# Decay differences of a Mamba-2 scan on GpSimd, one chunk ahead, with a third decay tile

## The chip, the core and the metric

One program on one core of one Trainium2 chip. The metric is the device time of one execution in microseconds, the median of several runs. The engines are named as in the profile: PE is TensorE, DVE is VectorE, ACT is ScalarE, POOL is GpSimd, SP is the engine that issues most DMAs. An engine works through its own queue in order; an instruction that waits holds up all that stands behind it on that engine.

## What is computed

A decoder of two layers over 2048 positions of width 1024: a Mamba-2 layer, then a layer of latent attention, with a final norm. The change lies in the chunked scan of the first layer (32 heads of 64 channels in 4 groups, 128 states, kernel chunks of 128 positions), cut from the reference to what matters:

```python
def step(state, inp):
    x_c, dt_c, B_c, C_c = inp
    cum = jnp.cumsum(dt_c * A_g, axis=1)
    seg = cum[:, :, None] - cum[:, None, :]
    L = jnp.exp(jnp.where(causal, seg, -jnp.inf))
    CB = jnp.einsum('btgn,bsgn->btsg', C_c, B_c)
    y_intra = jnp.einsum('btsg,btsgh,bsgh,bsghp->btghp', CB, L, dt_c, x_c)
    y_inter = jnp.einsum('btgn,bghpn,btgh->btghp', C_c, state, jnp.exp(cum))
    w_end = jnp.exp(cum[:, -1:] - cum) * dt_c
    new_state = state * jnp.exp(cum[:, -1])[..., None, None] + \
        jnp.einsum('bsgn,bsgh,bsghp->bghpn', B_c, w_end, x_c)
    return new_state, y_intra + y_inter
```

The kernel keeps the cumulated sums with the opposite sign. A decay tile holds, for one group and one chunk, the differences of 8 heads between each position (a partition) and each position (a column), clamped at zero, and then exp of minus that; the causal mask comes in through `CB`.

## The kernel before

The first layer runs over 4 blocks of 512 positions and, in each, over 4 groups; a group has 4 chunks of 128 positions, so there are 64 chunks. For one block and group there are three sweeps of matmuls over four PSUM banks each, all in fp16 pairs of a high and a low part, three matmuls a product: `xbc` (the inputs of the scan, with a convolution of width 4 that reads three columns of halo), `zgate` (the gate, in tiles `sz`) and `outp` (the output projection, one group later). The generator `ssd` makes the scan of one group. `mamba` runs the sweeps and, between their steps, 20 steps of `ssd`; the tile framework then puts the instructions in order by priority and its own model, and issues the waits. So a line's place in the code is not its place in an engine's queue.

What a sweep leaves in a PSUM bank has to be taken out before the next sweep may write there: for `xbc` ACT copies it to `craw` (L641), with the convolution behind (L645 on ACT, L647 on DVE, halo copies on POOL at L640 and L642); for `zgate` ACT makes a tanh (L670) and DVE multiplies (L671); for `outp` DVE adds into `hs` (L750).

In a chunk `ssd` does, as far as the change touches it:

- `decays` (L819) takes a tile `big` of 128 x 1024 fp32, of which there are two, and issues on SP the load of 8 rows of the cumulated sums, broadcast to all partitions (L825). The load for the next chunk is issued in the middle of a chunk.
- Eight operations on DVE (L893) subtract each position's own sum from the 128 columns of a head and clamp at zero.
- ACT makes the exponential of the whole tile (L897), DVE multiplies with `CB` (L898), and TensorE uses it in 32 small matmuls against `Xd` (L929). `Xd` is x times dt (DVE, L906).
- POOL makes the low halves of `Ct`, `Xp` and `Sp` (L846): `Ct` and `Xp` go into matmuls of the chunk, and `Sp`, the state, into those of the next chunk. DVE updates the state at L952 and L953.

Rows of a block's input come through `rows_in` (L596): two tiles `hx` of 128 x 1024 fp32 are loaded, normed, written as fp16 pairs into two more, and stored to `xp_d`; then the same for the other half. `fill` loads them back turned (eight transposing DMAs), and `steps` (L764 and behind) begins with matmuls on them. There are four `hx`. In the first block they also hold weights whose squares are summed (`scan`, through `later`), and `steps` takes one for itself.

Of the kernel before, what the change touches and what calls it, by code (L numbers as in the profile page):

```python
# [13 lines left out]
F16 = mybir.dt.float16  # L14
I32 = mybir.dt.int32
AF = mybir.ActivationFunctionType
ALU = mybir.AluOpType
# [4 lines left out]
P = 128  # L22
T = 2048
D = 1024
DI = 2048
G = 4
H = 32
# [3 lines left out]
NB = T // TB  # L31
KD = D // P
# [35 lines left out]
class Net:  # L68
# [273 lines left out]
    def mamba(self, cp):  # L342
# [7 lines left out]
        first = [self.t(self.sp, "big", [P, D], bufs=2) for _ in range(2)]  # L350
# [1 line left out]
        first += [self.t(self.sp, "yT", [P, D], bufs=4) for _ in range(4)]  # L352

        def later(kind):
            return self.t(self.hh, "hx", [P, D], bufs=4)

        def together(*parts):
            for group in zip_longest(*parts):
# [210 lines left out]
    def load_x(self, b, src):  # L569

        nc = self.nc
        self.xn[b] = xs = [self.t(self.hh, "hx", [P, D], bufs=4) for _ in range(4)]
        for i in range(4):
            nc.sync.dma_start(xs[i], src[i * P:(i + 1) * P, :])
        r = self.rows_rms(xs, [self.t(self.sp, "yt", [P, D], BF16, bufs=2) for _ in xs], D)
        for c in range(4):
            for i, x in enumerate(xs):
                v = x[:, c * D // 4:(c + 1) * D // 4]
                if i == 3:
                    nc.scalar.activation(v, v, AF.Copy, scale=r[:, i:i + 1])  # L580
                else:
                    nc.vector.tensor_scalar(v, v, r[:, i:i + 1], None, ALU.mult)
# [13 lines left out]
    def rows_in(self, b, src, tag="hx"):  # L596

        nc = self.nc
        for at in (0, 2 * P):
            xs = [self.t(self.hh, tag, [P, D], bufs=4) for _ in range(2)]  # L600
            for i, x in enumerate(xs):
                nc.sync.dma_start(x, src[at + i * P:at + (i + 1) * P, :])
            yield
            r = self.rows_rms(xs, [self.t(self.sp, "yt", [P, D], BF16, bufs=2) for _ in xs], D)
            up = self.t(self.sm, "rx", [P, 2], bufs=2)
            nc.vector.tensor_scalar(up, r, XSCALE, None, ALU.mult)
            us = [self.t(self.hh, tag, [P, KD, 2, P], F16, bufs=4) for _ in range(2)]
            for i, (x, u) in enumerate(zip(xs, us)):
                self.pair16(u[:, :, 0], u[:, :, 1], x.rearrange("p (k c) -> p k c", k=KD), up[:, i:i + 1])
            yield  # L610
            for i, u in enumerate(us):
                nc.sync.dma_start(self.xp_d[b][at + i * P:at + (i + 1) * P, :], u.rearrange("p k n c -> p (k n c)"))
# [144 lines left out]
    def steps(self, b):  # L757

        nc, v, xT = self.nc, self.nc.vector, self.xT[b]
        ps = self.t(self.pp, "tr", [P, TB], bufs=4)  # L760

        for k in range(KD):
            for n in range(2):
                nc.tensor.matmul(ps[0:2 * H, :], self.wdt[:, k].rearrange("p n h -> p (n h)"), xT[k][:, n, :],  # L764
                                 start=k + n == 0, stop=k + n == KD)
        wk = self.t(self.hh, "hx", [P, D], bufs=4)
        rt = self.t(self.sp, "yt", [2 * H, TB], bufs=2)
        nc.scalar.activation(rt, ps[0:2 * H, :], AF.Copy, scale=self.dtdown[0:2 * H])
        ps = self.t(self.pp, "tr", [P, TB], bufs=4)
# [4 lines left out]
        raw, e, q, p, dA, cT = (wk[:, n * P:n * P + P] for n in range(6))  # L774
# [44 lines left out]

    def decays(self, b, g, c):  # L820

        at, h0 = 16 * b + 4 * g + c, c * H + g * 8
        if at not in self.decay:
            E = self.decay[at] = self.t(self.sp, "big", [P, D], bufs=2)
            self.nc.sync.dma_start(E, self.dtv[b][5][h0:h0 + 8, :].rearrange("h t -> (h t)").partition_broadcast(P))  # L825
            return E
        return self.decay.pop(at).rearrange("p (h t) -> p h t", h=8)

    def ssd(self, b, g):

# [32 lines left out]
        for c in range(4):  # L863
            s = slice(c * P, (c + 1) * P)
            h0 = c * H + g * 8
# [11 lines left out]
                v.tensor_tensor(v8(t), v8(pi), heads(ecum), ALU.mult)  # L877
                return t

            if not (b or g or c):  # L880
                self.decays(0, 0, 0)
            E = self.decays(b, g, c)
            pb = self.t(self.pp, "tr", [P, TB], bufs=4)
            nc.tensor.transpose(pb[:, 0:P], BT[:, s], self.ident)
            nc.tensor.matmul(pb[:, P:2 * P], BT[:, s], CT[:, s], start=True, stop=True)
# [3 lines left out]
                Ct = halves(pair("Ct", P, 2), CT[:, s])  # L889
            CB = self.t(self.sp, "CB", [P, P], bufs=2)  # L890
            v.tensor_tensor(CB, pb[:, P:2 * P], self.triu, ALU.mult)
            for h in range(8):
                v.tensor_scalar(E[:, h, :], E[:, h, :], cum[:, h0 + h:h0 + h + 1], 0.0, ALU.subtract, ALU.max)  # L893
            after = 16 * b + 4 * g + c + 1
            if after < 16 * NB:
                self.decays(after // 16, after // 4 % 4, after % 4)
            act(E, E, AF.Exp, scale=-1.0)  # L897
            v.tensor_tensor(E, E, CB.unsqueeze(1).to_broadcast([P, 8, P]), ALU.mult)  # L898
            yield
# [12 lines left out]
            for h in range(8):  # L912
                hc = slice(h * 64, (h + 1) * 64)
                act(y[:, hc], px[:, hc], AF.Copy, scale=self.Dsk[:, g * 8 + h:g * 8 + h + 1])
            yield
            if b > 1 and c:
                yield
# [23 lines left out]
            yield  # L941
            if b == 1 and c:
                yield
            if not last:
                pst = self.t(self.pp, "tr", [P, TB], bufs=4)
                self.mm3(pst, Bt[:, 0], Bt[:, 1], Xp[:, 0], Xp[:, 1], True, True)
                if first:
                    st = self.state[g] = self.t(self.sp, f"st{g}", [P, TB], bufs=1)
                    v.tensor_copy(st, pst)
                else:  # L950
                    st = self.state[g]
                    v.tensor_tensor(v8(st), v8(st), heads(dec), ALU.mult)  # L952
                    v.tensor_tensor(st, st, pst, ALU.add)  # L953
                if c < 3:
                    old = halves(pair("Sp", TB, 1), st)
# [746 lines left out]
```

## Time and profile before

| | |
|---|---|
| median of 3 runs | 2904.24 us (2898.55 to 2908.7) |
| the profiled execution | 2901.06 us, its span 2899.3 us |
| the chip's granted TensorE clock | 0.992 of full speed |
| weights, input and start | 0 to 100 us |
| the scan with its projections | 100 to 1515 us |
| the second layer's projections | 1515 to 2010 us |
| attention | 2010 to 2620 us |
| last heads and output | 2620 to 2900 us |

The stages are cut by hand where the mix of work changes. POOL is busy for 301.57 us of the 1415 us of the scan, ACT for 878.65. A busy TensorE row counts a matmul from its start to its modelled end, and these overlap, so idle time is what a reader can trust. Idle time of another engine costs nothing by itself: it counts where TensorE waits for that engine.

### The profile page before, as it was taken

The page shows a single profiled execution, that of the slowest core. Times are in us where ns is not written, and L with a number is a line of the kernel's source. Part 1 is how long each engine was busy: PE and PEld are TensorE (multiplying, and loading weights), DVE is VectorE, ACT ScalarE, POOL GpSimd, SP SyncE. Part 2 cuts the span into 40 slices and gives each one's busy share as a digit, 9 for nine tenths or more (in the row PEclk, how much of TensorE's full clock was granted, in tenths as well). Part 3 has the DMA queues.
Part 4 walks back from the last instruction along what each step waited for, and adds up shares of the span by engine and source line. Part 5 has one row for each costly group of instructions (what it writes and reads, how often), then busy time and mean ns, then how long its engine had stood idle before and what let it go on. Part 6 is the DMA issues. An engine that isn't in the chain of part 4 may idle for free. (4 is left out here: it accounts for less than half of the span.)

```text
span 2899.3 us, 58091 instructions
## 1 busy us (share of the span) xinstructions
PE 2796.2 (96%) x21166; PEld 1621.4 (56%) x21166; DVE 2112.2 (73%) x5123; ACT 1801.4 (62%) x3900; POOL 853.5 (29%) x984
## 2 busy tenths in 40 slices
PE   7899999999999999998999999999999999998998
PEld 3455466544454454454455545555666666665787
DVE  6789877787777888788876355357777777778454
ACT  8767745576556665556554334234888888888522
POOL 0111212122122221123221122223665665665300
PEclk9999999999999999999999999999999999999999
DMA  8756636566665677647766877862212223223453
GB/s 287 258 191 202 217 116 194 166 197 170 203 208 163 194 201 225 215 143 211 229 143 232 269 217 230 243 200 78 70 50 67 65 53 73 68 64 89 164 200 109
DMA packets 358755, 483.33 MB, mean 167 GB/s; under 512 B 180162, under 2 KB 221922, under 8 KB 357028
## 3 DMA queue, kind: packets, MB, share of 16 engines
q1 hardware_dynamic: 347332, 443.70, 51.0%
q0 software_dynamic: 11136, 35.92, 3.5%
q8 instruction: 166, 2.72, 0.4%
q14 instruction: 121, 0.99, 0.1%
HBM read 332.83 MB, written 119.41 MB: 156 GB/s over the span
## 5 line engine op out<-in xcount | busy, mean ns | idle before, releaser
L1406 POOL TENSOR_TENSOR PTs<-x,PTs 128x512 f16<-128x512 f32 (+1 forms) x380 | 439.1, 1179 | 261.7 <-ACT PTs L1393 171.7
L1388 ACT ACTIVATE x<-s 128x512 f32<-128x512 f32 (+3 forms) x640 | 326.4, 524 | 48.7 <-PE s L1384 30.5
L84 PE MATMUL mm<-xT,wsp 128*128 128x512 f16 x800 | 306.1, 383 | 3.5 <-ACT wsp L115 3.3
L85 PE MATMUL mm<-xT,wsp 128*128 128x512 f16 x800 | 305.6, 382 | 0.0
L86 PE MATMUL mm<-xT,wsp 128*128 128x512 f16 x800 | 304.5, 381 | 0.2 <-DVE wsp L116 0.2
L1393 ACT ACTIVATE PTs<-x 128x1024 f16<-128x1024 f32 (+1 forms) x320 | 297.1, 929 | 9.4
L1271 DVE CUSTOM_DVE_ANT_0 junk<-s,fence,mx 128x512 bf16<-128x512 f32 (+1 forms) x372 | 242.1, 651 | 43.3 <-PE s L1269 3.0
L1423 PE MATMUL o<-K,PTs 128*128 128x65 f16 x2176 | 261.9, 192 | 2.0 <-POOL PTs L1406 1.5
L1421 PE MATMUL o<-K,PTs 128*128 128x64 f16 x2176 | 263.1, 192 | 0.0
L1422 PE MATMUL o<-K,PTs 128*128 128x65 f16 x2176 | 262.9, 194 | 0.0
L84 PE MATMUL mm<-wsp,xT 128*128 128x512 f16 (+1 forms) x640 | 231.9, 363 | 10.9 <-ACT craw L641 8.9
L85 PE MATMUL mm<-wsp,xT 128*128 128x512 f16 (+1 forms) x640 | 232.9, 364 | 3.3 <-DVE wsp L116 3.3
L846 POOL TENSOR_TENSOR Xp<-Xw,Xp 128x512 fp32r<-128x512 f32 x64 | 85.6, 1338 | 503.5 <-ACT Xp L845 346.4
L1421 PEld LDWEIGHTS <-PTs 128*128 128x128 f16 x2176 | 204.3, 96 | 52.2 <-issue 4.4
L86 PE MATMUL mm<-wsp,xT 128*128 128x512 f16 (+1 forms) x640 | 232.7, 364 | 0.0
L1422 PEld LDWEIGHTS <-PTs 128*128 128x128 f16 x2176 | 202.3, 97 | 52.8
L647 DVE SCALAR_TENSOR_TENSOR cacc<-craw,pack,cacc 128x512 f32<-128x512 f32 x288 | 213.7, 769 | 16.3 <-ACT cacc L645 15.1
L1382 PE MATMUL s<-xT,K 98*128 98x512 f16 (+1 forms) x628 | 218.5, 348 | 5.0 <-DVE mx L1271 3.9
L1383 PE MATMUL s<-xT,K 96*128 96x512 f16 (+1 forms) x628 | 218.3, 348 | 0.0
L1269 PE MATMUL s<-K,xT 96*128 96x512 f16 (+1 forms) x616 | 212.2, 347 | 6.1 <-DVE mx L1271 4.3
L1384 PE MATMUL s<-xT,K 96*128 96x512 f16 (+1 forms) x628 | 216.9, 345 | 0.0
L84 PE MATMUL mm<-wsp,yT 128*128 128x512 f16 (+1 forms) x512 | 199.9, 390 | 15.5 <-DVE sz L671 14.5
(476 smaller groups left out, 7111.5 us busy)
## 6 DMA issues: line engine op xcount, KB each, us to landing
wsp<-wi_d SPq DMA_DIRECT2D x96, 512.0 KB
big<-cumT SPq DMA_DIRECT2D x64, 512.0 KB
wraw<-in_ssm_w_out_dram SPq DMA_DIRECT2D x96, 256.0 KB
wi_d<-wsp SPq DMA_DIRECT2D x32, 512.0 KB
wsp<-wo_d SPq DMA_DIRECT2D x32, 512.0 KB
wsp<-wu_d SPq DMA_DIRECT2D x28, 512.0 KB
hx<-in_ssm_w_in_dram SPq DMA_DIRECT2D x48, 256.0 KB
wraw<-in_ssm_w_in_dram SPq DMA_DIRECT2D x48, 256.0 KB
```

The lines of the kernel that those rows point to most:

```text
L84: mm(out, l_hi, r_hi, start=start, stop=False)
L85: mm(out, l_hi, r_lo, start=False, stop=False)
L86: mm(out, l_lo, r_hi, start=False, stop=stop)
L1271: self.nc.vector.tensor_tensor_reduce(junk[:, :w], s[:, :w], fence[:, at:at + w], -1.0 / MSCALE, peak[:, i - 1, j:j + 1] if i else 3.0e38, ...
L1382: mm(s, K[0:98, 0, ks], Q[0:98, 0, c], start=True, stop=False)
L1383: mm(s, K[0:96, 0, ks], Q[0:96, 1, c], start=False, stop=False)
L1388: act(o, s, AF.Exp)
L1393: act(u[:, 0, at:end], x[:, at:end], AF.Copy)
L1406: engine.tensor_tensor(u[:, 1, a:b], x[:, a:b], u[:, 0, a:b], ALU.subtract)
L1421: mm(o[:, 0:64], hi, V[:, k, 0:64], start=k == 0 and j == 0, stop=False, skip_group_check=True)
L1422: mm(o[:, 0:65], hi, V[:, k, 64:129], start=False, stop=False, skip_group_check=True)
L1423: mm(o[:, 0:65], lo, V[:, k, 64:129], start=False, stop=k == 4 * qb + j, skip_group_check=True)
```

## The change

Three things change together.

1. `decays` takes a tile for chunk n, counted through all blocks and groups, from `big` (two tiles) or, for each third chunk, from a new tag `hE` (one tile). So there are three decay tiles in turn.
2. The eight differences go from DVE to POOL, into `differences`. The code calls it for the next chunk: four heads in the second step of the current chunk, four in its fourth. For the first chunks of block 0 and group 0 it is called at the start.
3. The space of `hE` comes from `hx`, which goes from four tiles to three. `load_x` takes three `hx` and the `hE`. `rows_in` allocates its output tiles one by one, so that the second can take the buffer of the first input.

```diff
         def later(kind):
-            return self.t(self.hh, "hx", [P, D], bufs=4)
+            return self.t(self.hh, "hx", [P, D], bufs=3)
...
-        self.xn[b] = xs = [self.t(self.hh, "hx", [P, D], bufs=4) for _ in range(4)]
+        self.xn[b] = xs = [self.t(self.hh, "hx", [P, D], bufs=3) for _ in range(3)]
+        xs.append(self.t(self.hh, "hE", [P, D], bufs=1))
...
         for at in (0, 2 * P):
-            xs = [self.t(self.hh, tag, [P, D], bufs=4) for _ in range(2)]
+            n = 3 if tag == "hx" else 4
+            xs = [self.t(self.hh, tag, [P, D], bufs=n) for _ in range(2)]
...
-            us = [self.t(self.hh, tag, [P, KD, 2, P], F16, bufs=4) for _ in range(2)]
-            for i, (x, u) in enumerate(zip(xs, us)):
+            us = []
+            for i, x in enumerate(xs):
+                u = self.t(self.hh, tag, [P, KD, 2, P], F16, bufs=n)
+                us.append(u)
...
     def decays(self, b, g, c):
 
-        at, h0 = 16 * b + 4 * g + c, c * H + g * 8
-        if at not in self.decay:
-            E = self.decay[at] = self.t(self.sp, "big", [P, D], bufs=2)
-            self.nc.sync.dma_start(E, self.dtv[b][5][h0:h0 + 8, :].rearrange("h t -> (h t)").partition_broadcast(P))
-            return E
-        return self.decay.pop(at).rearrange("p (h t) -> p h t", h=8)
+        h0 = c * H + g * 8
+        E = self.t(self.hh, "hE", [P, D], bufs=1) if (16 * b + 4 * g + c) % 3 == 2 else \
+            self.t(self.sp, "big", [P, D], bufs=2)
+        E = self.decay[b, g, c] = E.rearrange("p (h t) -> p h t", h=8)
+        self.nc.sync.dma_start(E.rearrange("p h t -> p (h t)"),
+                               self.dtv[b][5][h0:h0 + 8, :].rearrange("h t -> (h t)").partition_broadcast(P))
+
+    def differences(self, b, g, c, heads):
+
+        E, cum, h0 = self.decay[b, g, c], self.dtv[b][1], c * H + g * 8
+        for h in heads:
+            self.nc.gpsimd.tensor_scalar(E[:, h, :], E[:, h, :], cum[:, h0 + h:h0 + h + 1], 0.0, ALU.subtract, ALU.max)
...
-            if not (b or g or c):
-                self.decays(0, 0, 0)
-            E = self.decays(b, g, c)
+            if first and g == 0:
+                self.decays(b, g, c)
+                self.differences(b, g, c, range(8))
+            after = 16 * b + 4 * g + c + 1
+            after = (after // 16, after // 4 % 4, after % 4) if after < 16 * NB else None
+            E = self.decay.pop((b, g, c))
...
-            for h in range(8):
-                v.tensor_scalar(E[:, h, :], E[:, h, :], cum[:, h0 + h:h0 + h + 1], 0.0, ALU.subtract, ALU.max)
-            after = 16 * b + 4 * g + c + 1
-            if after < 16 * NB:
-                self.decays(after // 16, after // 4 % 4, after % 4)
+            if after:
+                self.decays(*after)
             act(E, E, AF.Exp, scale=-1.0)
...
                 act(y[:, hc], px[:, hc], AF.Copy, scale=self.Dsk[:, g * 8 + h:g * 8 + h + 1])
+            if after:
+                self.differences(*after, range(4))
             yield
...
             if b == 1 and c:
                 yield
+            if after:
+                self.differences(*after, range(4, 8))
```

What this makes of the engines' queues shows at one place, the end of `zgate` for block 2, group 2, while the scan is at group 1 (about 903 to 911 us of the profile). The numbers behind a name are the framework's; `big_10206` is one decay tile, that of chunk 1 of group 1, in both programs. DVE before, from a late difference to the first eviction of `sz`:

```order
L893 TENSOR_SCALAR big_10206<-big_10206,d_cum_8132 128x128
L245 SCALAR_TENSOR_TENSOR rsq_10143<-rsx_10129,rss_10141 128x4
L967 TENSOR_SCALAR pw_9176<-pw_9176 128x4
L893 TENSOR_SCALAR big_10206<-big_10206,d_cum_8132 128x128
L247 SCALAR_TENSOR_TENSOR rsy_10145<-rsq_10143,rsy_10139 128x4
L243 TENSOR_TENSOR rss_10147<-rsy_10145 128x4
L245 SCALAR_TENSOR_TENSOR rsq_10149<-rsx_10129,rss_10147 128x4
L247 SCALAR_TENSOR_TENSOR rsy_10151<-rsq_10149,rsy_10145 128x4
L968 SCALAR_TENSOR_TENSOR rr_10153<-rsy_10151,wod,pw_9176 128x4
L671 SCALAR_TENSOR_TENSOR sz_10091<-sz_10091,mm_9910 128x512
```

In the changed program the same small operations stand there without the differences. ACT at the same place before, and then the piece of its queue where this tile's exponential (L897 before, L907 now) stands after the change:

```order
L532 ACTIVATE yt_10107,hs_9439<-wraw_10002,pack 128x32
L115 ACTIVATE y_10062<-y_9940,pw_9176 128x4x128
L897 ACTIVATE big_10206<-big_10206 128x1024
L670 ACTIVATE sz_10091<-mm_9910,half 128x512
L670 ACTIVATE sz_10100<-mm_9911,half 128x512
```

```order
L645 ACTIVATE craw_9876<-mm_9639,down 128x512
L532 ACTIVATE yt_10010,hs_9439<-wraw_9928,pack 128x32
L907 ACTIVATE big_10206<-big_10206 128x1024
L653 ACTIVATE xs_9834<-cacc_9829 128x512
L645 ACTIVATE craw_9894<-mm_9640,down 128x512
```

The exponential of the tile has moved from ahead of the evictions of `sz` to ahead of the last eviction of `craw`, one sweep earlier. (Before, the exponential of the tile before it, `big_9866`, stands at that place.) POOL before and now, where the differences of this tile come:

```order
L846 TENSOR_TENSOR Xp_9672<-Xw_9661,Xp_9672 128x512
L846 TENSOR_TENSOR Ct_10193<-BC_9630,Ct_10193 128x128
L846 TENSOR_TENSOR Sp_9787<-st_197_1104,Sp_9787 128x512
L642 COPY halo<-craw_9817 128x3
L642 COPY halo<-craw_9835 128x3
```

```order
L856 TENSOR_TENSOR Xp_9672<-Xw_9661,Xp_9672 128x512
L856 TENSOR_TENSOR Ct_10201<-BC_9630,Ct_10201 128x128
L837 TENSOR_SCALAR big_10206<-big_10206,d_cum_8140 128x128 x8
L856 TENSOR_TENSOR Sp_9795<-st_197_1112,Sp_9795 128x512
L646 COPY halo<-craw_9825 128x3
```

All eight differences stand together, between `Ct` of one chunk and `Sp` of the chunk before it, and ahead of the halo copies.

More of the change, by code (lines that the diff above doesn't have):

```diff
@@ L765, in steps @@
                                  start=k + n == 0, stop=k + n == KD)
-        wk = self.t(self.hh, "hx", [P, D], bufs=4)
+        wk = self.t(self.hh, "hx", [P, D], bufs=3)
         rt = self.t(self.sp, "yt", [2 * H, TB], bufs=2)
```

## The prediction

> **What bounds the kernel now.** I read the busy shares first, then the same by stage, then the waits of TensorE (PE) in the one stage that the change touches.
>
> ```profile
> span 2899.3 us, 58091 instructions
> PE 2796.2 (96%) x21166; PEld 1621.4 (56%) x21166; DVE 2112.2 (73%) x5123; ACT 1801.4 (62%) x3900; POOL 853.5 (29%) x984
> ```
> ```profile
> core 0: us, PE busy (x) PEld busy (x) DVE busy (x) ACT busy (x) POOL busy (x), PEclk, DMA share, GB/s
> 0.00:100.00 100.00, 77.57 (x386) 39.17 (x387) 68.89 (x216) 77.53 (x160) 6.18 (x22) 0.97 0.85 280
> 100.00:1515.00 1415.00, 1361.85 (x8075) 726.92 (x8074) 1147.55 (x2562) 878.65 (x2282) 301.57 (x362) 0.99 0.63 191
> 1515.00:2010.00 495.00, 487.37 (x2641) 253.30 (x2640) 261.93 (x611) 188.97 (x343) 101.11 (x163) 1.00 0.70 217
> ```
>
> TensorE is the bound everywhere. The scan lies between 100 and 1515 us; there TensorE is idle for 1415 − 1361.85 = 53.2 us, and VectorE (DVE) is 81% busy. So whatever happens to VectorE, the scan can give back at most 53 us, 1.8% of the kernel. What that idle time waits for, in the same window:
>
> ```profile
> PE mm L84 <- DVE sz L671: 14.5, 9, 4.7
> PE mm L84 <- ACT craw L641: 9.1, 7, 2.8
> PE tr L764 <- DMA xT<-xp_d: 4.3, 3, 2.6
> PE tr L929 <- DVE big L898: 4.3, 2, 3.3
> PE tr L929 <- DVE Xd L906: 3.7, 4, 1.7
> ```
>
> Each row gives us in total, how often, and the longest. The first two are PSUM banks that the next sweep needs and that ScalarE (ACT) and VectorE have not emptied; the last two are the scan's own operands. The work that moves, and what waits for it:
>
> ```profile
> L893 DVE TENSOR_SCALAR big<-big,d_cum 128x128 f32<-128x128 f32 x496 | 137.4, 319 | 34.0 <-DMA big<-cumT 33.8
> ```
> ```profile
> ACT big L897 <- DVE big L893: 32.1, 16, 3.7
> ```
>
> The differences hold VectorE for 137.4 us and make it stand for another 34.0 us until a decay tile has landed; ScalarE's exponential waits 32.1 us for them. One of the nine `sz` stalls shows how this reaches TensorE. VectorE, ScalarE, then TensorE:
>
> ```profile
> 907.34 0.28 DVE L893 TENSOR_SCALAR big<-big,d_cum 128x128 f32<-128x128 f32 x1
> 907.68 0.28 DVE L893 TENSOR_SCALAR big<-big,d_cum 128x128 f32<-128x128 f32 x1
> ...
> 909.70 1.88 DVE L671 SCALAR_TENSOR_TENSOR sz<-sz,mm 128x512 f32<-128x512 f32 x3 [0.83 <-ACT sz L670]
> ```
> ```profile
> 905.86 0.70 ACT L115 ACTIVATE y<-y,pw 128x512 f16<-128x512 f32 x1
> 908.04 1.06 ACT L897 ACTIVATE big<-big 128x1024 f32<-128x1024 f32 x1 [1.48 <-PE mm L86]
> 909.00 2.40 ACT L670 ACTIVATE sz<-mm,half 128x512 f32<-128x512 f32 x4
> ```
> ```profile
> 910.45 0.38 PE L84 MATMUL mm<-wsp,yT 128*128 128x512 f16 x1 [1.25 <-DVE sz L671]
> ```
>
> The last difference ends at 907.96, the exponential starts at 908.04, and the four evictions stand behind it in ScalarE's queue. The row names a matmul as what ended the exponential's wait, but the difference ended 0.08 us before it, so I put it down to the difference. ScalarE was free from 906.56: without the exponential in the way the first eviction could start up to 2.44 us earlier, which is more than the stall of 1.25 us.
>
> **The change part by part.** The order shown with the change says where things stand. VectorE loses all 512 differences. In the example the exponential of the same tile (`big_10206`) stood between the last difference and the evictions of `sz`; now it stands one sweep earlier, ahead of the last `craw` eviction, and the evictions of `sz` have nothing of it before them. The exponential of the tile before stood in that other place already, so the `craw` evictions get no additional 1.06 us.
>
> On GpSimd (POOL) eight differences now stand ahead of `Sp` and of the halo copies. For `Sp` wait the next chunk's matmul and VectorE's state update, for the copies ScalarE's convolution:
>
> ```profile
> DVE st L952 <- POOL Sp L846: 18.3, 14, 2.1
> ```
>
> The price of a difference on GpSimd is not in the trace; the nearest rows:
>
> ```profile
> L846 POOL TENSOR_TENSOR Ct<-BC,Ct x58: 447/457/938, 120.4 to 1485.8; 128x128 fp32r<-128x128 f32 x58
> L642 POOL COPY halo<-craw x90: 177/226/2541, 103.2 to 1440.9; 128x3 f32<-128x3 f32 x90
> ```
> ```profile
> L893 DVE TENSOR_SCALAR big<-big,d_cum x496: 268/279/1362, 100.3 to 1495.8; 128x128 f32<-128x128 f32 x166
> ```
> ```profile
> L846 POOL TENSOR_TENSOR Sp<-st,Sp 128x512 fp32r<-128x512 f32 x60 | 82.9, 1382 | 229.7 <-ACT Sp L845 227.4 <-PE mm L86 2.3
> ```
>
> Columns of the first three: shortest, median, longest in ns. A copy of three columns (177) is the floor, the same shape with two inputs (457) the likely ceiling; a difference reads one tensor, so I take 0.4 us, nearer to the equal shape. Eight make 3.2 us, all 512 make 205 us on an engine that is idle for 1113 of 1415 us. GpSimd waits 229.7 us for 60 `Sp`, 3.8 us each: the run fits into the wait that it is put in front of. If the cover is gone (1.4 us a piece, the longest `L893`), a run takes 11 us and everything behind it is late: that is the slower rival.
>
> *Gain.* Of the 14.5 us for `sz` I take four fifths, 12: the cause stands ahead of the evictions in the order before and is gone from it now. Of the 9.1 us for `craw` a third, 3: VectorE's freed time speeds the convolution that frees the buffers, but the exponential still stands there. Of the 4.3 + 3.7 us at L929 half, 4. Sum 19; bounds 0 (another engine takes over each wait) and 32 (all four rows).
>
> *Contention.* VectorE's differences are usually 0.28 us but reach 1.36, and GpSimd's three-column copies go from 0.18 to 2.54: the two engines hold each other up.
>
> ```profile
> L647 DVE SCALAR_TENSOR_TENSOR cacc<-craw,pack,cacc x270: 730/744/1798, 105.7 to 1448.3; 128x512 f32<-128x512 f32 x135
> ```
> ```profile
> L647 DVE SCALAR_TENSOR_TENSOR cacc<-craw,pack,cacc 128x512 f32<-128x512 f32 x270 | 200.3, 770 | 15.3 <-ACT cacc L645 14.4
> L898 DVE TENSOR_TENSOR big<-big,CB 128x1024 f32<-128x1024 f32 x63 | 76.8, 1219 | 0.7
> ```
>
> L647's mean lies 770 − 744 = 26 ns above its median, 7 us in all, and L893's 319 − 279 = 40 ns, 20 us. The first grows with GpSimd's load, the second goes. At worst each of 512 differences stops VectorE for its 0.4 us whenever it runs an operation that can be stopped. For that share I take half (L647, L893 and L898 alone are 414 of 1415 us, 29%): 102 us. At best nothing. I take 35 us. VectorE's net gain is then 137.4 + 34.0 − 35 = 136 us. At the rate of the gain (19 us of TensorE's time for 171 of VectorE's, 0.11) the 35 us cost 4; bounds 0 and 11.
>
> [...]
>
> *The third tile.* A load no longer waits until the chunk before has been multiplied:
>
> ```profile
> SPq L825 <- PE tr L929: 85.6, 48, 4.5
> ```
>
> These 85.6 us of the DMA queue are off TensorE's path (its waits above name no weight load in that place), so I count nothing for them; they are what lets the differences run early. In exchange the input rows have three buffers for four. `rows_in` can fetch its second pair only as the first is written out, which delays `xp_d` and the 4.3 us that TensorE waits at L764. Bounds 0 and 6 (doubling it and half as much again); I take 1, since eight transposes and several weight loads stand between. In the first 100 us the scans of the weights have three buffers too; TensorE is idle 22.4 us there, and I take 1, bounds 0 and 5.
>
> *Sum*: −19 + 4 + 1 + 1 = −13. The profiled execution took 2901.06 us, so 2888; it lies 3.2 us under the median 2904.24 of runs from 2898.55 to 2908.7, which would give 2891. I predict 2889. Bounds of the terms: −32 and +22.
>
> **The rivals.** *Nothing to tell*: the two engines hold each other up in every run of differences, and the stalls change owner. VectorE then loses the 102 us of the worst case, 11 us for TensorE; of the gain only the 12 us for `sz` are left, since ScalarE goes on waiting for y and Xd, which the change does not touch; the buffers cost 2. −12 + 11 + 2 = +1: 2902. [...] For it: the long rows of `L893` and of the copies. Against it: 362 operations of GpSimd in the scan have lengthened `L647` by 7 us only, and in the example nothing but differences and exponential stood in the way.
>
> ```profile
> ACT yt L935 <- DVE y L933: 127.7, 53, 4.8
> ACT Xw L910 <- DVE Xd L906: 108.2, 52, 5.4
> ```
>
> *Slower*: GpSimd's queue becomes the bound at the place shown. At 1.4 us a difference, a run takes 11.2 us, 7.4 more than the 3.8 that hide it, and `Sp`, the halo copies and the exponential are late in 64 chunks; the exponential holds up the last `craw` eviction. 64 × 7.4 = 474 us at the rate of 0.11 are 52 us, and 2888 + 52 = 2940. It decides from about 0.7 us a difference (5.6 − 3.8 = 1.8 us late, 13 us in all), where the gain is used up. For it: the 2541 ns copy. Against it: the tile is multiplied a whole chunk later, so lateness has room.
>
> *More*: all of the 32 us come back, contention is nil and the buffers cost 1: 2870. The order shows the differences gone, so that the change does not do what it says is excluded.
>
> **How the numbers follow.** Forecast 0.55 (its own range 2877 to 2898), nothing to tell 0.27, slower 0.14, more 0.04. 0.3% is 8.7 us, about what a measurement of this kernel can tell: faster means under 2895.5, slower over 2912.9. The forecast's upper end reaches over 2895.5 for a small part that goes to "within", the part of the first rival below 2895.5 balances it. Faster 0.57, within 0.27, slower 0.16. The range for 8 in 10 runs from 2868 to 2914; it takes in the rival without effect and leaves out most of the slower one.
>
> **What would show it.** Right: no VectorE differences, its busy time in the scan some 100 us lower; GpSimd's differences at 0.3 to 0.6 us; the wait for `sz` at 3 us or so; ScalarE's wait for the differences near zero; TensorE's idle time in the scan near 40 us. Wrong: differences over 0.7 us, ScalarE's exponential waiting for GpSimd, VectorE's state update waiting for `Sp` well above its 18 us, or L647 far above 770 ns.

## The result, and the profile after

The changed kernel takes 3108.86 us (median of 4 runs, 3102.76 to 3114.05); the kernel before, beside it, 2902.64 us. The ratio is 1.0708 (95% interval 1.0679 to 1.0736): 206 us or 7% slower, far outside the predicted range.

The page of the changed kernel, its span and its busy times:

```profile
span 3109.1 us, 58146 instructions
PE 2852.7 (92%) x21166; PEld 1637.4 (53%) x21166; DVE 2009.6 (65%) x4611; ACT 1802.6 (58%) x3900; POOL 1232.9 (40%) x1496
```

VectorE is busy for 2009.6 us in place of 2112.2: the 100 us that the prediction wanted off VectorE are off, and they bought nothing. The span grew by 209.8 us. TensorE's idle time went from 2899.3 − 2796.2 = 103.1 us to 3109.1 − 2852.7 = 256.4, 153.3 more; and its 21166 matmuls, the same number, are busy 56.5 us longer. The two make the 209.8. By stage (columns as before; the scan now ends near 1725 us):

```profile
core 0: us, PE busy (x) PEld busy (x) DVE busy (x) ACT busy (x) POOL busy (x), PEclk, DMA share, GB/s
100.00:1725.00 1625.00, 1423.55 (x8140) 746.18 (x8141) 1057.38 (x2094) 887.75 (x2312) 663.91 (x852) 0.95 0.54 168
1725.00:2220.00 495.00, 490.96 (x2631) 254.63 (x2629) 261.60 (x610) 188.72 (x340) 101.34 (x163) 0.99 0.69 217
```

The scan holds nearly all of it: 1625 us in place of 1415, 201.5 us of it without TensorE in place of 53.2, and a granted clock of 0.95 there in place of 0.99. The stage behind it takes 495 us as before. The longest of what TensorE waits for in the scan, and the row of the input (us in all, times, longest):

```profile
PE mm L84 <- ACT craw L645: 57.5, 26, 8.2
PE mm L84 <- DVE sz L675: 40.2, 12, 8.4
PE tr L941 <- DVE Xd L916: 20.8, 13, 5.8
PE mm L84 <- DVE CB L904: 14.5, 1, 14.5
PE tr L768 <- DMA xT<-xp_d: 5.6, 3, 3.3
```

The two waits that the change was to shorten, `craw` and `sz`, went from 9.1 and 14.5 us to 57.5 and 40.2. The single wait of 14.5 us stands at the start of the scan (88.1 to 102.5 us); for most of it ScalarE stands in front of the exponential of the third tile (11.09 us in all) until GpSimd has made its differences. The transposed input (`xp_d`), for which the cut of the input buffers was a danger, is at 5.6 us after 4.3. Who holds up ScalarE, GpSimd and VectorE, in three answers of the list of waits:

```profile
ACT big L907 <- POOL big L837: 156.2, 33, 9.2
ACT hE L907 <- POOL hE L837: 78.9, 16, 8.1
```
```profile
POOL big L837 <- DMA big<-cumT: 90.5, 26, 7.6
POOL hE L837 <- DMA hE<-cumT: 48.3, 14, 5.8
```
```profile
DVE st L966 <- POOL Sp L856: 175.3, 43, 9.1
```

ScalarE stands for 235 us in front of the exponential until GpSimd has made the differences. GpSimd itself stands for 139 us until a decay tile has landed, with `Sp` behind the differences in its queue; VectorE waits 175.3 us for `Sp`, after 18.3. And the price (shortest, median, longest in ns):

```profile
L837 POOL TENSOR_SCALAR big<-big,d_cum x344: 704/714/2034, 70.8 to 1682.9; 128x128 f32<-128x128 f32 x172
L837 POOL TENSOR_SCALAR hE<-hE,d_cum x168: 707/714/1581, 90.9 to 1661.2; 128x128 f32<-128x128 f32 x168
```

A difference takes GpSimd 714 ns, on VectorE it took 279.

One place shows the whole chain. SP, GpSimd, ScalarE, VectorE and TensorE of the changed kernel, 1295 to 1311 us:

```profile
1295.87 0.36 SPq L830 DMA_DIRECT2D big<-cumT  x1
```
```profile
1301.89 5.55 POOL L837 TENSOR_SCALAR big<-big,d_cum 128x128 f32<-128x128 f32 x8 [5.72 <-DMA big<-cumT]
1307.41 1.27 POOL L856 TENSOR_TENSOR Sp<-st,Sp 128x512 fp32r<-128x512 f32 x1
```
```profile
1300.67 0.71 ACT L115 ACTIVATE y<-y,pw 128x512 f16<-128x512 f32 x1
1307.47 1.06 ACT L907 ACTIVATE big<-big 128x1024 f32<-128x1024 f32 x1 [6.10 <-POOL big L837]
1308.43 0.60 ACT L115 ACTIVATE wraw<-wraw,gains 128x384 f16<-128x384 f32 x1
1308.94 0.67 ACT L645 ACTIVATE craw<-mm,down 128x512 f32<-128x512 f32 x1
```
```profile
1300.19 0.15 DVE L952 TENSOR_SCALAR pw<-pwe 128x1 int32<-128x1 int32 x1
1308.71 0.69 DVE L966 TENSOR_TENSOR st<-st,d_dec 128x512 f32<-128x512 f32 x1 [8.36 <-POOL Sp L856]
```
```profile
1301.05 0.38 PE L86 MATMUL mm<-xT,wsp 128*128 128x512 f16 x1
1309.66 0.58 PE L84 MATMUL mm<-wsp,xT 128*128 128x512 f16 x1 [8.23 <-ACT craw L645]
1310.04 0.63 PE L85 MATMUL mm<-wsp,xT 128*128 128x512 f16 x1
```

The load is issued at 1295.87 and GpSimd can begin at 1301.89. Eight differences take 5.55 us. ScalarE had come to the exponential at 1301.37 and stands there for 6.10 us, with the eviction of `craw` behind it; that eviction starts at 1308.94, and TensorE, which needs the bank, stands still for 8.23 us. Of these, 2.1 us are the exponential, the operation behind it and the eviction themselves (1307.47 to 1309.61), and the other 6.10 are the wait. On the other side `Sp` starts as the last difference ends, and VectorE waits 8.36 us for it. When TensorE goes on, its matmuls take 0.63 us in place of 0.38. The windows around the stall:

```profile
1295.00:1301.00 6.00, 6.00 (x31) 2.91 (x29) 4.75 (x10) 2.61 (x7) 0.69 (x1) 1.00 0.95 306
1309.60:1313.70 4.10, 4.04 (x10) 1.43 (x10) 4.10 (x8) 3.34 (x7) 1.14 (x4) 0.50 0.56 129
```

The granted clock is 1.00 before the stall and 0.50 for the first 4.1 us after it, so this stall is paid a second time. The same shows over the whole kernel: by the clock's records in the two traces TensorE was busy for 40 us at 0.50 before and for 143 us after, and half of these 103 us more is 52 us, nearly all of the 56.5 us of longer busy time. A stall's length alone does not tell whether the clock falls: in the same trace one of 2.3 us, near 676 us, was followed by 0.50 (678.9 to 682.3 us), and one of 3.3 us, near 247 us, by 1.00 (250.2 to 254 us).

### The profile page after: what moved, and what is told of

The parts are those of the page before. It is cut to its first block, busy times and chain, and to the rows that moved or that the text cites. A ratio compares the mean times of both kernels' runs of the same rounds, so it can differ in the third digit from the quotient of the medians.

```text
span 3109.1 us, 58146 instructions
## 1 busy us (share of the span) xinstructions
PE 2852.7 (92%) x21166; PEld 1637.4 (53%) x21166; DVE 2009.6 (65%) x4611; ACT 1802.6 (58%) x3900; POOL 1232.9 (40%) x1496
## 4 chain that ended last, share of the span: by engine, by line
PE 40%; DVE 4%; ACT 3%; DMA 2%; POOL 2%; issue 2%; SPq 0%; DVEq 0%; ACTq 0%; POOLq 0%
PE s L1396 4%; PE s L1397 4%; PE s L1398 3%; PE s L1283 3%; PE mm L84 3%; PE mm L85 3%; PE mm L86 3%; PE tr L85 3%; PE tr L86 3%; PE tr L84 3%; PE o L1436 2%; PE o L1437 2%; PE o L1435 2%; POOL big L837 1%; DMA os<-gate_d 1%
## 5 line engine op out<-in xcount | busy, mean ns | idle before, releaser
L84 PE MATMUL mm<-xT,wsp 128*128 128x512 f16 x800 | 311.9, 390 | 46.6 <-ACT craw L645 20.5
L85 PE MATMUL mm<-xT,wsp 128*128 128x512 f16 x800 | 310.6, 388 | 0.0
L86 PE MATMUL mm<-xT,wsp 128*128 128x512 f16 x800 | 309.1, 387 | 0.5 <-DVE wsp L116 0.5
L837 POOL TENSOR_SCALAR big<-big,d_cum 128x128 f32<-128x128 f32 x344 | 261.0, 776 | 120.4 <-DMA big<-cumT 90.5
L84 PE MATMUL mm<-wsp,xT 128*128 128x512 f16 (+1 forms) x640 | 234.4, 367 | 38.7 <-ACT craw L645 38.2
L84 PE MATMUL mm<-wsp,yT 128*128 128x512 f16 (+1 forms) x512 | 207.1, 404 | 53.3 <-DVE sz L675 40.2
L85 PE MATMUL mm<-wsp,xT 128*128 128x512 f16 (+1 forms) x640 | 235.5, 368 | 9.9 <-DVE wsp L116 9.9
L86 PE MATMUL mm<-wsp,xT 128*128 128x512 f16 (+1 forms) x640 | 235.2, 368 | 0.0
L1397 PE MATMUL s<-xT,K 96*128 96x512 f16 (+1 forms) x628 | 218.8, 348 | 0.0
```

Of the source, the lines that this page charges most:

```text
L84: mm(out, l_hi, r_hi, start=start, stop=False)
L85: mm(out, l_hi, r_lo, start=False, stop=False)
L86: mm(out, l_lo, r_hi, start=False, stop=stop)
L1397: mm(s, K[0:96, 0, ks], Q[0:96, 1, c], start=False, stop=False)
```

## The experiments

Each time is given as its ratio to the kernel before, run beside it on the same chip (2898 to 2903 us).

### Which part of the change

Four kernels take the parts apart. Theory A: the price of the differences reaches ScalarE's exponential and what stands behind it. B: the third tile and the cut buffers. C: the queue on GpSimd, above all `Sp`.

The changed kernel with the differences back on VectorE:

```diff
-            self.nc.gpsimd.tensor_scalar(E[:, h, :], E[:, h, :], cum[:, h0 + h:h0 + h + 1], 0.0, ALU.subtract, ALU.max)
+            self.nc.vector.tensor_scalar(E[:, h, :], E[:, h, :], cum[:, h0 + h:h0 + h + 1], 0.0, ALU.subtract, ALU.max)
```

> The changed kernel with only the engine put back: three decay tiles, three hx buffers, the differences one chunk ahead in the code, but on VectorE. Theory A (price: a difference takes GpSimd 0.71 us, eight in a row 5.8 us, and ScalarE's exponential stands right behind them): the loss goes, 2880 to 2915 us, and ScalarE's wait for the differences falls from 235 us to under 40. Theory B (tile: the third tile moves the exponential ahead to a place where its load is not there yet, and three hx buffers delay the input): the engine does not matter, still over 3050 us. Theory C (queue: Sp and the copies wait behind the differences on GpSimd, whatever one of them costs): about 2900, VectorE's wait for Sp back from 175 to about 20 us.

Measured 2910.11 us, 1.0041 (1.0026 to 1.0056). ScalarE's waits for differences are 35.6 us.

The kernel before with three `hx` for four and nothing else of the change (the diff is shortened):

```diff
-        self.xn[b] = xs = [self.t(self.hh, "hx", [P, D], bufs=4) for _ in range(4)]
+        self.xn[b] = xs = [self.t(self.hh, "hx", [P, D], bufs=3) for _ in range(3)]
+        xs.append(self.t(self.hh, "hE", [P, D], bufs=1))
```

> The kernel before with only the buffers of the input rows cut from four to three (the fourth tile of the first block under a name of its own); differences and decay tiles as before. Theory A and C: 2900 to 2915 us, at most 6 us lost as the prediction bounds it. Theory B: a good part of the 206 us shows here, over 2930.

Measured 2900.32 us, 1.0006 (0.9997 to 1.0015).

The kernel before with the engine of the differences changed and nothing else:

```diff
             for h in range(8):
-                v.tensor_scalar(E[:, h, :], E[:, h, :], cum[:, h0 + h:h0 + h + 1], 0.0, ALU.subtract, ALU.max)
+                nc.gpsimd.tensor_scalar(E[:, h, :], E[:, h, :], cum[:, h0 + h:h0 + h + 1], 0.0, ALU.subtract, ALU.max)
```

> The kernel before with only the engine of the differences changed to GpSimd: two decay tiles, four hx, the call at its old place in the code. Theory A: as slow as the changed kernel or slower, 3050 to 3200 us, since eight differences of 0.71 us stand between the load and the exponential with one tile less in hand. Theory B: within 20 us of 2903. Theory C: slower by less than the changed kernel, 2930 to 3050, since the code now has them behind Sp of the chunk before.

Measured 3108.4 us, 1.0731 (1.071 to 1.0752): the whole loss, without the third tile and without "one chunk ahead". The two waits are those of the changed kernel: ScalarE's exponential waits 238.6 us for GpSimd's differences and VectorE 176.1 for `Sp`.

The changed kernel with every other head on VectorE:

```diff
-            self.nc.gpsimd.tensor_scalar(E[:, h, :], E[:, h, :], cum[:, h0 + h:h0 + h + 1], 0.0, ALU.subtract, ALU.max)
+            (self.nc.gpsimd if h % 2 else self.nc.vector).tensor_scalar(E[:, h, :], E[:, h, :], cum[:, h0 + h:h0 + h + 1], 0.0, ALU.subtract, ALU.max)
```

> The changed kernel with every other head's difference on VectorE, so that GpSimd has four in a tile for eight. Theory A: the run on GpSimd takes 2.9 us, VectorE does its four beside it, and the loss shrinks by more than half: 2920 to 3010 us. Theory B: nothing changes, 3080 to 3110. Theory C: Sp still waits behind a run on GpSimd, 3000 to 3080.

Measured 2949.04 us, 1.0176 (1.0159 to 1.0194): half the differences cost a quarter of the loss.

B falls: the engine alone makes the loss. The rest of the change, with the differences on VectorE, is not free either (0.4% slower, where the cut of the buffers alone cannot be told from no change), but that is 12 us of 206.

### Through which exit

GpSimd does the same work, but on a scratch tile, which has the space of the third decay tile (the diff is shortened):

```diff
-        E = self.t(self.hh, "hE", [P, D], bufs=1) if (16 * b + 4 * g + c) % 3 == 2 else \
-            self.t(self.sp, "big", [P, D], bufs=2)
+        E = self.t(self.sp, "big", [P, D], bufs=2)
...
-        E, cum, h0 = self.decay[b, g, c], self.dtv[b][1], c * H + g * 8
+        E, cum, h0 = self.scratch, self.dtv[b][1], c * H + g * 8
```

> The changed kernel with its 512 GpSimd operations done on a scratch tile that nothing else reads (two decay tiles, the scratch in place of the third), while the exponential takes the loaded sums as they are: GpSimd has the same work at the same places of the code, nobody waits for its result. The differences are left out of what is computed. Theory A (what costs is that ScalarE's exponential, in order, waits for GpSimd, and all evictions behind it): 2880 to 2910 us. Theory C (Sp and the halo copies wait behind the differences on GpSimd): 2950 to 3060, VectorE's wait for Sp still over 100 us. Theory D (the two engines block each other's access): 2910 to 2950, with VectorE's two-input operations well over their usual 0.74 us.

Measured 3174.27 us, 1.0955 (1.0934 to 1.0975), outside what any of the theories expected. What TensorE waited for in its scan:

```profile
PE tr L85 <- POOL Xp L855: 191.2, 7, 38.7
PE mm L84 <- DVE sz L675: 14.5, 9, 4.1
PE mm L84 <- ACT craw L645: 8.1, 7, 2.8
```

This experiment failed as a test. The operations on the scratch need nothing but `d_cum`, which is there for a whole block at once; so they stood in GpSimd's queue in long rows (the longest 66 operations, 47.3 us), and `Xp` behind such a row kept TensorE waiting 38.7 us at a time. It does show what an in-order queue can do to an operand that TensorE needs. One thing in it bears on A all the same: nobody waited for GpSimd's results, and the two eviction waits stood where they were in the kernel before (14.5 and 9.1 us).

What it is worth to VectorE to be rid of the work: the kernel before without the eight differences.

```diff
-            for h in range(8):
-                v.tensor_scalar(E[:, h, :], E[:, h, :], cum[:, h0 + h:h0 + h + 1], 0.0, ALU.subtract, ALU.max)
```

> The kernel before with the differences left out altogether (the exponential takes the loaded sums): the most that taking them off VectorE can bring. If the prediction's gain term was right, 19 us less: 2875 to 2890. If what VectorE does here is not on the path, 2893 to 2903.

Measured 2892.97 us, 0.9982 (0.997 to 0.9993): 5 us (2 to 9 by the interval), not 19. TensorE's wait for `sz` in that kernel:

```profile
PE mm L84 <- DVE sz L671: 14.3, 9, 4.3
```

It was 14.5 us with the differences on VectorE. They are gone and the wait stays: it has another owner. At the place of the prediction's example (890 to 915 us of the profile) TensorE does not wait any more, but elsewhere it waits longer.

The prices, from operations at the end of the kernel before, with nothing beside them (they lengthen the program, so its time tells nothing). The first of three loops, where `d4` and `s4` stand for the tiles seen as four heads:

```diff
+        for n in range(8):
+            po.tensor_scalar(d[:, 0:P], s[:, 0:P], m[:, 0:1], 0.0, ALU.subtract, ALU.max)
+            po.tensor_scalar(d[:, 0:P], s[:, 0:P], m[:, 0:1], None, ALU.subtract)
+            po.tensor_scalar(d[:, 0:P], s[:, 0:P], 1.0, 0.0, ALU.subtract, ALU.max)
+            po.tensor_tensor(d[:, 0:P], s[:, 0:P], s[:, P:2 * P], ALU.subtract)
+            po.tensor_copy(d[:, 0:P], s[:, 0:P])
+            po.tensor_scalar(d, s, m[:, 0:1], 0.0, ALU.subtract, ALU.max)
+            po.tensor_tensor(d4, s4, m[:, 0:4].unsqueeze(2).to_broadcast([P, 4, P]), ALU.subtract)
```

> The kernel before with a row of GpSimd operations at its very end, where nothing else runs, for their prices: the change's form (128 x 128, a scalar from a tile, two operations), with one operation, with two constants, two input tensors, a copy, 128 x 512; then the change's form beside VectorE operations with two inputs, and beside VectorE operations with one. Price theory: the change's form takes 0.70 us by itself, alone too. Lock theory: alone about 0.4, the rest comes from VectorE at work beside it. The two-input form about 0.45 as in the scan.

The seven in the order of the diff; then the change's form 24 times beside VectorE operations with two inputs; then 24 times with VectorE's operations of one input, which go on beside the first twelve only:

```profile
L1626 POOL TENSOR_SCALAR pb_d<-pb_s,pb_m x8: 712/712/722, 2889.1 to 2933.5; 128x128 f32<-128x128 f32 x8
L1627 POOL TENSOR_SCALAR pb_d<-pb_s,pb_m x8: 605/605/606, 2889.9 to 2934.3; 128x128 f32<-128x128 f32 x8
L1628 POOL TENSOR_SCALAR pb_d<-pb_s x8: 642/642/643, 2890.6 to 2935.0; 128x128 f32<-128x128 f32 x8
L1629 POOL TENSOR_TENSOR pb_d<-pb_s x8: 452/452/453, 2891.3 to 2935.7; 128x128 f32<-128x128 f32 x8
L1630 POOL COPY pb_d<-pb_s x8: 289/289/290, 2891.8 to 2936.2; 128x128 f32<-128x128 f32 x8
L1631 POOL TENSOR_SCALAR pb_d<-pb_s,pb_m x8: 1992/1992/1992, 2892.2 to 2936.6; 128x512 f32<-128x512 f32 x8
L1632 POOL TENSOR_TENSOR pb_d<-pb_s,pb_m x8: 1038/1038/1039, 2894.3 to 2938.7; 128x512 f32<-128x512 f32 x8
L1636 POOL TENSOR_SCALAR pb_d<-pb_e,pb_m x24: 712/712/1266, 2940.3 to 2959.4; 128x128 f32<-128x128 f32 x24
L1640 POOL TENSOR_SCALAR pb_d<-pb_s,pb_m x12: 950/952/1092, 2960.6 to 2972.3; 128x128 f32<-128x128 f32 x12
L1640 POOL TENSOR_SCALAR pb_d<-pb_s,pb_m x12: 712/712/712, 2973.3 to 2982.2; 128x128 f32<-128x128 f32 x12
```
```profile
2960.57 12.50 DVE L1641 TENSOR_SCALAR pb_f<-pb_s,pb_m 128x512 f32<-128x512 f32 x24
```

The change's form takes 712 ns with nothing beside it, so that is its own price, and 0.4 alone with the rest from VectorE falls. Beside VectorE's operations with two inputs its median stays at 712 (the longest is 1266); beside those with one input it takes 950, and 712 again as soon as VectorE is done. So VectorE's one-input operations of 128 x 512 do hold GpSimd up, by 240 ns a difference, but that comes on top of the price. VectorE's own operations beside the differences took 486 to 488 ns with one input and 751 to 771 with two. Alone, the form is dearer than an operation with two input tensors (452) and 2.5 times a copy (289); one operation in place of two saves 107 ns, constants in place of a scalar from a tile 70. Subtracting a repeated column from 512 columns at once takes 1038 ns, 260 for 128 columns.

The changed kernel with the low halves of `Sp` made by VectorE (the diff is shortened; `low` is true for `Sp` alone):

```diff
-            nc.gpsimd.tensor_tensor(u[:, 1], x, u[:, 0].bitcast(F32), ALU.subtract)
+            (v if low else nc.gpsimd).tensor_tensor(u[:, 1], x, u[:, 0].bitcast(F32), ALU.subtract)
```

> The changed kernel with the low halves of Sp made by VectorE, so that GpSimd's run of differences has no Sp behind it. Theory A: 3040 to 3110 us, ScalarE still waits over 150 us for differences. Theory C: most of the loss goes, 2920 to 3000 us.

Measured 3046.28 us, 1.0515 (1.0485 to 1.0546). ScalarE's waits in it:

```profile
ACT big L907 <- POOL big L837: 155.1, 39, 7.0
ACT hE L907 <- POOL hE L837: 80.8, 16, 7.0
```

Without `Sp` behind the run 58 us of the 206 come back, though VectorE has the work of `Sp` now; ScalarE goes on waiting as before. So both exits cost. That can be tested with all work left where it is, by order alone.

### The same work in another order

Two rules, in a construct of the framework that puts an instruction behind a named one on the same engine. *Late*: the exponential behind the square of the chunk before, so that ScalarE comes to it when the differences are done.

```diff
+            with self.tc.issue_after(self.square) if self.square else nullcontext():
                 act(E, E, AF.Exp, scale=-1.0)
...
-            act(junk, y, AF.Square, scale=0.5 * 512.0 ** -0.5, accum_out=ms[:, c:c + 1])
+            self.square = act(junk, y, AF.Square, scale=0.5 * 512.0 ** -0.5, accum_out=ms[:, c:c + 1]).ins
```

> The changed kernel with one rule of order more: on ScalarE the exponential of a chunk stands behind the square of the chunk before (a chunk later than now, still ahead of its use). All work is the same. After the four runs before I hold that the run of differences costs at two exits: the exponential that stands in front of the evictions (theory A, some 145 of the 206 us) and Sp behind it on GpSimd (theory C, some 62, what the kernel with Sp on VectorE gained). So 2930 to 2990 us, ScalarE's wait for differences under 50 us. If only the queue on GpSimd counted (C alone): 3060 to 3110. If blocked accesses did it (D): over 3060 too.

Measured 2973.84 us, 1.0250 (1.0235 to 1.0265). Of ScalarE's waits for differences one of 5.0 us is left. VectorE's for `Sp` is:

```profile
DVE st L968 <- POOL Sp L857: 184.2, 43, 8.5
```

*Behind*: the differences behind `Sp` of the chunk before (`kept` is true for `Sp` alone).

```diff
+        with self.tc.issue_after(self.low) if self.low else nullcontext():
+            for h in heads:
+                self.nc.gpsimd.tensor_scalar(E[:, h, :], E[:, h, :], cum[:, h0 + h:h0 + h + 1], 0.0, ALU.subtract, ALU.max)
...
+            low = nc.gpsimd.tensor_tensor(u[:, 1], x, u[:, 0].bitcast(F32), ALU.subtract).ins
+            if kept:
+                self.low = low
```

> The changed kernel with the other rule of order: on GpSimd the differences of the next chunk stand behind Sp of the chunk before, which they stood ahead of. The exponential is left free. A and C with the shares named: VectorE's wait for Sp falls from 175 to under 60 us, ScalarE's wait stays over 150, 3030 to 3090 us. C alone: 2900 to 2960. A alone: 3090 to 3130.

Measured 3139.66 us, 1.0824 (1.0808 to 1.084), slower than the changed kernel and not the 3030 to 3090 expected. ScalarE's waits:

```profile
ACT big L911 <- POOL big L839: 236.2, 38, 9.0
ACT hE L911 <- POOL hE L839: 121.0, 20, 7.6
```

They rose from 235 to 357 us. VectorE's wait for `Sp` did fall, to 54.6 us: what `Sp` no longer waits, the differences wait, and the exponential in front of the evictions with them.

Both rules, the two diffs together:

> Both rules of order in the changed kernel, the same work on the same engines. A and C: nearly all comes back, 2895 to 2930 us, which is the time with the differences on VectorE (2910) give or take. If a cost remains that no order removes (D, the engines blocking each other, or GpSimd short of time): over 2950.

Measured 2913.43 us, 1.0043 (1.0026 to 1.006).

| | exponential free | exponential late |
|---|---|---|
| differences free | 1.0708 (the changed kernel) | 1.0250 |
| differences behind `Sp` | 1.0824 | 1.0043 |

The same instructions on the same engines cost 206 us in one order and 12 in another. The shares don't add: the second rule loses 32 us alone, and gains 60 where the exponential is late.

The price, without touching the order: one subtraction for all eight heads on GpSimd, the clamp on ScalarE.

```diff
-            for h in range(8):
-                v.tensor_scalar(E[:, h, :], E[:, h, :], cum[:, h0 + h:h0 + h + 1], 0.0, ALU.subtract, ALU.max)
+            nc.gpsimd.tensor_tensor(E, E, cum[:, h0:h0 + 8].unsqueeze(2).to_broadcast([P, 8, P]), ALU.subtract)
...
+            act(E, E, AF.Relu)
             act(E, E, AF.Exp, scale=-1.0)
```

> The kernel before with the subtraction of all eight heads in one GpSimd operation of two inputs (128 x 1024, the second a column repeated) and the clamp on ScalarE ahead of the exponential. By the prices measured at the end of a kernel (1.04 us for 512 columns) GpSimd needs 2.1 us a tile in place of 5.7. Price theory: about as the kernel with four of eight heads on GpSimd or better, 2905 to 2950 us. If it is the place on GpSimd and not the price: over 3000.

Measured 2937.92 us, 1.0119 (1.01 to 1.0139), with 2.02 us a tile on GpSimd. So a cheaper run loses far less at an untouched place. It is not a clean comparison of price, as ScalarE has 64 clamps more.

### The last 12 us, and the gain by itself

Both rules, but two decay tiles and four `hx` as before (the diff is shortened, and against the kernel with both rules):

```diff
-        E = self.t(self.hh, "hE", [P, D], bufs=1) if (16 * b + 4 * g + c) % 3 == 2 else \
-            self.t(self.sp, "big", [P, D], bufs=2)
+        E = self.t(self.sp, "big", [P, D], bufs=2)
```

> The differences on GpSimd with both rules of order, but with the two decay tiles and four hx of the kernel before. If the last 12 us come from the third tile and what it moves (as the kernel with three tiles and the differences on VectorE suggests, which lost 12 too): 2893 to 2905 us, no difference from before, or up to 5 us better, the bound that the kernel without differences gave. If they come from GpSimd (its price, or the engines blocking each other): 2908 to 2925. If two tiles are too few for the slower run of differences: over 2925.

Measured 2910.7 us, 1.0035 (1.0023 to 1.0046). The third tile is not needed for the rest of the loss: 10 us are there without it. With both rules GpSimd's and VectorE's operations meet more often. The groups of the kernel with both rules and three tiles (busy us, mean ns):

```profile
L839 POOL TENSOR_SCALAR big<-big,d_cum 128x128 f32<-128x128 f32 x344 | 323.4, 956 | 3.5 <-DMA hx<-in_ssm_w_in_dram 3.5
L839 POOL TENSOR_SCALAR hE<-hE,d_cum 128x128 f32<-128x128 f32 x168 | 152.3, 923 | 0.0
```
```profile
L652 DVE SCALAR_TENSOR_TENSOR cacc<-craw,pack,cacc 128x512 f32<-128x512 f32 x288 | 226.8, 816 | 41.1 <-ACT cacc L650 40.3
```

A difference takes 923 to 956 ns on the mean there, over 200 more than alone and about what it took beside VectorE's one-input operations, and VectorE's convolution 816, after 769 before. In the changed kernel, where the engines mostly stood waiting for each other, it had 775:

```profile
L651 DVE SCALAR_TENSOR_TENSOR cacc<-craw,pack,cacc 128x512 f32<-128x512 f32 x288 | 214.3, 775 | 46.5 <-ACT cacc L649 45.5
```

That would fit the two engines holding each other up, but no run took that away alone, so the 10 us are not shown to come from it.

The kernel before with only the rule *late*, the first of the two diffs (differences on VectorE):

> The kernel before with one rule: ScalarE's exponential behind the square of the chunk before; differences on VectorE, two tiles. The prediction's gain step says that the exponential in front of the evictions of sz costs most of the 14.5 us that TensorE waits for them: then 2885 to 2895 us. If the wait for sz only changes its owner, as it did when the differences were left out (14.3 us): 2896 to 2906.

Measured 2891.23 us, 0.9969 (0.9957 to 0.998), 9 us faster than before beyond the interval. TensorE's waits (L85 is here what was L84):

```profile
PE mm L85 <- DVE sz L672: 10.9, 8, 3.5
PE mm L85 <- ACT craw L642: 12.3, 8, 3.5
```

`sz` fell from 14.5 to 10.9 us and `craw` rose from 9.1 to 12.3, so that the two together went from 23.6 to 23.2. The time lies in the range that the prediction's step asked for, but the step does not make it: what `sz` gains `craw` loses. TensorE's idle time over the whole kernel fell from 103.1 to 94.6 us, by small amounts in many rows; through which of them the order pays is open. It pays with no work moved to another engine, and this kernel beats the kernel before as well as the changed one. It is also the nearer comparison for the kernel with both rules and two tiles, which ran beside it: 2910.7 against 2891.23 us. The exponential is late in both; the differences on GpSimd, called earlier and behind `Sp`, go with 19 us.

## Why the prediction was wrong

The step that failed is the cost of coming late. The sum has no term for a run of differences that is late at the exponential and at `Sp`; the changed kernel waits 235 us at the one and 175 at the other, and order alone, which takes most of both away (5.0 and 57.9 us are left), brings the loss from 206 us to 12. The terms one by one:

**The price of a difference** was too low. I took 0.4 us and called the operation of equal shape with two inputs (457 ns) the likely ceiling, since a difference reads one tensor. It takes 712 alone. This does not make the loss yet: by the rival's own sum a run of 5.7 us is 1.9 us late and costs 13 us in all, which would have used up the gain and no more, where 206 us were lost. The row I leaned on was of another form of instruction: on GpSimd the difference with its one input tensor took 712 ns alone, where a subtraction of two took 452, and on VectorE the difference took 279.

**"The run fits into the wait that it is put in front of"** did not hold. GpSimd's 3.8 us in front of `Sp` are a mean of time in which nothing had to be done. The run does not start when GpSimd is free, but when its load has landed (139 us of waiting in the scan), and `Sp` became ready meanwhile. VectorE's 34 us of waiting for loads, which I booked as a gain, moved to GpSimd and grew fourfold.

**The exponential in front of the evictions** is the step that cost most. The order was read rightly: it stands ahead of the last `craw` eviction. I put its cost there at nothing, since another had stood in that place before. What counts is when its input is ready, and for that the sum has no term. Before, VectorE finished the differences about when ScalarE came to the exponential (32.1 us of waits in the scan); from GpSimd they come up to 9.2 us late, and every eviction behind waits too. The new place is not needed for it, as the kernel with the engine alone changed shows (238.6 us of waits, 1.0731). With the exponential later in order, 134 us of the 206 returned.

**The price of the rival "slower"** was sized wrongly, with the mechanism right. I turned lateness into time at 0.11 us of TensorE's per us, a rate got from VectorE's busy time, and came to 2940 even for 1.4 us a difference. A late instruction in front of evictions does not work by such a rate: in the example all 6.10 us of ScalarE's wait went into TensorE's stall of 8.23, with half a clock behind it. The chance of 0.14 for it was too low as well: of the four signs named as "wrong", three are there (over 0.7 us, ScalarE waiting for GpSimd, VectorE waiting for `Sp`); only the convolution's mean kept still.

**The gain** of 19 us was 5 in the kernel without the differences, less than the 8.7 us that the prediction named as what can be told. The example was read rightly, as its stall is gone there, but I took it for the cause of four fifths of the `sz` stalls; without the differences the wait had another owner, the rival's "stalls change owner".

**The rest.** The cut of the input buffers was priced at 1 us, bounds 0 and 6; it measured within noise (1.0006). The contention term (+4) was priced as VectorE being stopped for 0.4 us by half of the differences, which no run shows. In the changed kernel the convolution's mean kept still (775); what the probe shows is GpSimd being held up, beside VectorE's one-input operations (950 ns for 712). With the waits gone both engines' means rise, but what that costs is not shown. The third tile, priced at nothing, and the earlier call go with a loss of 12 us where the differences stay on VectorE; through which wait is open.

## What to carry to other kernels

An instruction moved to another engine is priced by its form on that engine, measured, and not by the nearest shape. Then look at what consumes it in order: where the consumer stands ahead of work that frees PSUM banks, lateness can go to TensorE whole, as in the example (6.10 us, in a stall of 8.23), and cost more through its clock (0.50 for 4.1 us there). And before moving work, leave it out in one run: here that would have said that 5 us were to be had, while an order alone gave 9.

## What the runs showed of the hardware that was not expected

On GpSimd a one-input operation with a scalar from a tile and two operations took 712 ns for 128 x 128, where two input tensors took 452 and a copy 289; for 512 columns it was 1992 against 1038 for a subtraction with a repeated column. Beside VectorE's one-input operations of 128 x 512 GpSimd's 712 ns became 950, beside two-input operations the median stayed at 712 (longest 1266).

After a stall of 8.23 us TensorE's granted clock was 0.50 for the next 4.1 us (matmuls of 0.63 us in place of 0.38), and after one of 2.3 us for 3.4 us; after one of 3.3 us it was 1.00. Over the kernel 153.3 us more of idle time came with 56.5 us of longer busy time, about a third as much again, 52 of them by the clock's records.
